# Prefix log-sum-exp over a sequence: all loads and stores issued by ScalarE instead of SyncE

## The chip, the cores and the metric

The kernel runs on one core of one Trainium2 chip. The metric is the device time of one execution in microseconds (us). The core has engines that each work through an instruction list of their own: TensorE (PE, with its weight loads as PEld), VectorE (DVE), ScalarE (ACT), GpSimd (POOL) and SyncE (SP). Transfers between the chip's memory (DRAM) and the buffers on the core are issued by an engine and carried out by 16 DMA engines. All numbers come from the times of whole executions and from one execution taken by the hardware profiler.

## The reference

For an input `x` of shape 4 x 4096 x 4128 (batch, sequence, features; float32), the output at each place is the logarithm of the sum of the exponentials of all inputs up to that place in the sequence:

```python
out[:, 0, :] = x[:, 0, :]
for t in range(1, S):
    mx = np.maximum(out[:, t - 1, :], x[:, t, :])
    out[:, t, :] = mx + np.log(np.exp(out[:, t - 1, :] - mx) + np.exp(x[:, t, :] - mx))
```

Input and output are 270.5 MB each.

## The kernel before

The kernel takes Exp of the input, makes a running sum over the sequence, and takes Ln of it. If a running sum leaves the safe range, a flag sends it to a slow general version (`_general`), which the profiled execution does not enter.

**Steps.** The sequence of each batch is cut into steps of `P * r` = 128 x 3 or 128 x 2 rows: each of the 128 partitions holds `r` consecutive rows of 4128 features. There are 45 steps, numbered 0 to 44 here (`n = 45`); 38 have three rows (6192 KB in and as much out) and seven have two (4128 KB): steps 0, 16, 27, 37, 39, 43 and 44. There are four buffers (`SLOTS = 4`); step t works in place in buffer t mod 4, so load t must wait until store t - 4 has landed.

**Chunks.** Each step is worked in three chunks of 1376 columns, 0 to 2. For a chunk, ScalarE takes Exp of all rows (`exp`, line 126); VectorE adds the rows of a partition (`sums`, lines 154 and 164); TensorE multiplies by a triangular matrix of ones, which gives each partition the sum over all partitions before it (`head`, line 172); VectorE adds that to the rows (`add`, lines 182, 188 and 197), and ScalarE takes Ln (`log`, lines 203, 207 and 208). What the steps before have summed up enters through the last partition, and for chunk 2 by `fold` (line 144).

**Order.** The order on each engine is written out by hand, under a manual schedule: `lists` holds one list of operations each for the moves, ScalarE (`act`), VectorE (`vec`) and TensorE (`pe`). `turns` says how many Exp of step t + 1 stand ahead of each Ln of step t. In most steps the ScalarE order is Ln chunk 0, two Exp of the next step, Ln chunk 1, the third Exp, Ln chunk 2. For step 40 all three Exp of step 41 stand ahead of the third Ln; after it come Ln of step 41 chunk 0, Exp of step 42 chunks 0 and 1, and so on.

**Moves.** The list `moves` (lines 228 to 237) is SyncE's: loads 0 to 3, store 0, store 1, load 4, store 2, load 5, and so on, store t followed by load t + 3; behind store 40 stand two loads, 43 and 44. A load is one transfer, except that loads 1, 2 and 3 (`BY_ROW`) are three each, one per row (line 107). This makes 96 transfers. The loop from line 345 to the end of the schedule emits the lists; `needs` says what an operation depends on, and `seen` which of its dependences an earlier wait has already covered. ScalarE's function tables are loaded at the start (line 37).

Of the kernel before, what the change touches and what calls it, by code (L numbers as in the profile page):

```python
# [13 lines left out]
MM = 512  # L14
NC = 3
SLOTS = 4
BY_ROW = (1, 2, 3)
PASSED = NC - 1
SMALL = 2.0 ** -63
LARGE = 2.0 ** 62  # L20
# [4 lines left out]
def kernel(  # L25
# [5 lines left out]
    nc = tc.nc  # L31
# [2 lines left out]
    CH = D // NC  # L34
    cuts = [(s, min(s + MM, CH)) for s in range(0, CH, MM)]

    nc.scalar.preload_act_table_set("natural_log_exp_and_others")
    consts = ctx.enter_context(tc.tile_pool(name="consts", bufs=1))
    zpool = ctx.enter_context(tc.tile_pool(name="zpool", bufs=1))
    xpool = ctx.enter_context(tc.tile_pool(name="xpool", bufs=1))  # L40
# [7 lines left out]
        out=below, in_=below, pattern=[[1, P]], compare_op=ALU.is_ge,  # L48
# [5 lines left out]
        out=carried, in_=below, pattern=[[0, P]], compare_op=ALU.not_equal,  # L54
# [4 lines left out]
        out=summed, in_=below, pattern=[[1, P]], compare_op=ALU.not_equal,  # L59
# [27 lines left out]
    made = {}  # L87

    def follows(inst, *ops):
        for op in ops:  # L90
            for other in made.get(op, ()):
                tc.declare_no_dep(inst.ins, other.ins, reason="a wait in between has seen it")

    class Step:
# [7 lines left out]

        def load(self):
            if self.n not in BY_ROW:
                return [nc.sync.dma_start(out=self.xt, in_=self.dram(x))]
            return [
                nc.sync.dma_start(out=self.xt[:, j, :], in_=self.dram(x)[:, j, :])
                for j in range(self.r)
            ]

        def store(self):
            return [nc.sync.dma_start(out=self.dram(out), in_=self.xt)]  # L112

    class Chunk:
        def __init__(self, step, c):
# [35 lines left out]
        def sums(self):  # L151
            r, e, got = self.t.r, self.row, []
            if r == 3:
                got.append(nc.vector.tensor_tensor(out=e[1], in0=e[0], in1=e[1], op=ALU.add))  # L154
                for free in () if self.passed else made.get(("log", self.t.n - 1, self.c), ()):
                    tc.add_manual_dep(
                        got[0].ins, free.ins.name,
                        mybir.DependencyInfo(
                            mybir.DependencyClass.Sync, mybir.DependencyReason.DATA,
                        ),  # L160
                        reason="the next sum writes what this Ln reads",
                    )
            n = P if self.passed else P - 1
            got.append(nc.vector.tensor_tensor(  # L164
                out=self.z[0:n], in0=e[r - 2][0:n], in1=e[r - 1][0:n], op=ALU.add,
            ))
            return got
# [46 lines left out]
    steps = []  # L214
# [10 lines left out]
        s.chunks = [Chunk(s, c) for c in range(NC)]  # L225
    n = len(steps)

    moves = [("load", t) for t in range(SLOTS)]
    ahead = SLOTS
    for t in range(n):  # L230
        moves.append(("store", t))
        if t and ahead < n:
            moves.append(("load", ahead))
            ahead += 1
            if ahead == n - 1:
                moves.append(("load", ahead))
                ahead += 1

    lists = {"move": moves, "act": [], "vec": [], "pe": []}
    act, vec, pe = lists["act"], lists["vec"], lists["pe"]  # L240
    usual_turn = (0, 2, 3, 3), (0, 0, 1, 1)
    alone = (0, 0, 0, 0)
# [15 lines left out]
    }  # L258
    given = {"exp": [0] * n, "sums": [0] * n}

    def exps(t, k):
        while t < n and given["exp"][t] < k:
            act.append(("exp", t, given["exp"][t]))
            given["exp"][t] += 1

    def passing(t):
        if t and steps[t - 1].last:
            vec.append(("total", t - 1, PASSED))
        if t < n:
            vec.append(("least" if steps[t].first else "fold", t, PASSED))  # L270

    def sums(t, k):
        while t < n and given["sums"][t] < k:
# [3 lines left out]
            if c == PASSED - 1 and t:  # L277
                passing(t)

    exps(0, 2)  # L280
    for t in range(n):
        ahead_exps, ahead_sums = turns.get(t, usual_turn)
        exps(t, NC)
        sums(t, 2)
        for c in range(NC):
            exps(t + 1, ahead_exps[c])
            act.append(("log", t, c))
            sums(t + 1, ahead_sums[c])
            vec.append(("add", t, c))
            if c == 0:  # L290
                sums(t, NC)
            pe.append(("head", t, c))
        exps(t + 1, ahead_exps[NC])
        sums(t + 1, ahead_sums[NC])
    passing(n)

    def needs(what, t, c=None):
        if what == "load":
            return [("store", t - SLOTS)]
        if what == "store":  # L300
            return [("log", t, c) for c in range(NC)]
        if what == "head":
            u, d = divmod(t * NC + c - 2, NC)
            need = [("sums", t, c), ("add", u, d)]
            if d == PASSED and u >= 0:
                need.append(("total", u, d) if steps[u].last else ("fold", u + 1, d))
            return need if c == PASSED else need + [("add", t - 1, c)]
        if what == "sums":
            need = [("exp", t, c)]
            if c != PASSED:  # L310
                return need + [("log", t - 1, c)]
            return need if steps[t].first else need + [("fold", t, c)]
        if what == "add":
            need = [("head", t, c)]
            return need + ([("least", t, PASSED)] if steps[t].first and t else [])
        return {
            "exp": [("load", t)],
            "fold": [("exp", t, c), ("head", t - 1, c)],
            "total": [("head", t, c)],
            "least": [("exp", t, c)],  # L320
            "log": [("add", t, c)],
        }[what]

    def seen(what, t, c=None):
        gone = [
            (op, u, d) for u in range(t % SLOTS, t, SLOTS) for d in range(NC)
            for op in ("exp", "least", "fold", "sums", "head", "add", "log")
        ]
        gone += [("load", u) for u in range(t % SLOTS, t, SLOTS)]
        gone += [("store", u) for u in range(t % SLOTS, t - SLOTS, SLOTS)]  # L330
        if what == "load":
            return gone
        gone.append(("store", t - SLOTS))
        if what == "exp":
            return gone
        gone.append(("load", t))
        if what == "store":
            gone += [(op, t, d) for d in range(NC) for op in ("exp", "least", "fold", "sums", "head", "add")]
        if what in ("head", "add", "log"):
            gone.append(("exp", t, c))  # L340
        if what in ("add", "log"):
            gone.append(("sums", t, c))
        return gone

    done, at = set(), {e: 0 for e in lists}
    while any(at[e] < len(l) for e, l in lists.items()):
        before = len(done), sum(at.values())
        for e, l in lists.items():
            while at[e] < len(l):
                op = l[at[e]]  # L350
                if op[1] < n:
                    if any(0 <= d[1] and d not in done for d in needs(*op)):
                        break
                    done.add(op)
                    of = steps[op[1]]
                    made[op] = getattr(of if len(op) == 2 else of.chunks[op[2]], op[0])()
                    for inst in made[op]:
                        follows(inst, *seen(*op))
                    if op[0] == "sums" and op[2] != PASSED:
                        for inst in made[op]:  # L360
                            follows(inst, *((o, op[1] - 1, op[2]) for o in ("sums", "head", "add")))
                        for inst in made[op][1:]:
                            follows(inst, ("exp", *op[1:]), ("log", op[1] - 1, op[2]))
                at[e] += 1
        assert before != (len(done), sum(at.values()))
# [3 lines left out]
        out=fits[:, :counts], in0=probe, scalar1=LARGE, scalar2=None, op0=ALU.is_le,  # L369
    )  # L370
    nc.vector.tensor_scalar(
        out=fits[0:1, counts:], in0=short, scalar1=SMALL, scalar2=None, op0=ALU.is_ge,
# [7 lines left out]
        out=flag, in0=good, scalar1=float(P), scalar2=None, op0=ALU.is_lt,  # L380
# [62 lines left out]
```

## Time and profile before

| what | value |
|---|---|
| time, median of 3 runs (lowest to highest) | 1260.25 us (1260.09 to 1260.42) |
| time of the profiled execution | 1259.65 us |
| its span, first to last instruction | 1257.9 us |
| DMA, mean over the span | 430 GB/s, 541.24 MB |
| busy DVE / ACT / PE | 1048.3 / 930.1 / 585.0 us |
| ACT waits for DVE `z`, line 207 | 168.1 us, 48 times |
| ACT waits for loads, line 126 | 124.1 us, 31 times, longest 11.0 |
| load of three rows, issue to landing, median | 40.1 us |
| store of three rows, issue to landing, median | 26.0 us |

The page has a line for each DMA queue (packets, MB, share of the 16 engines), and a map in which each digit is the busy share of one fortieth of the span in tenths. The chain of waits goes back from the last instruction, at each step to what released it. A row of the waits has the engine, its line, what it waited for, the total in us, the number of times and the longest. A row of the order of time has start and duration in us, engine, line, operation, output and input, the count of merged instructions, and in brackets the idle time before it and what ended that. A merged row's duration runs from the start of the first to the end of the last, with what lies between. "SPq" is SyncE's queue of transfers: the duration is that of the issue, not of the transfer.

### The profile page before, as it was taken

Reading aid. Unit: us, or ns where it says so; the run is one execution under the profiler, and the core shown is the slowest. Engines: PE = TensorE matmul, PEld = TensorE weight load, DVE = VectorE, ACT = ScalarE, POOL = GpSimd, SP = SyncE. Lnnn points to the kernel's source line nnn. Section 1 sums busy time; section 2 is a strip of 40 time slices with the busy share of each in tenths; the row PEclk is TensorE's granted clock in tenths of the full one; section 3 lists DMA queues with packets and bytes.
Section 4 is the critical chain, followed back from the end, with each engine's and each line's share of the span. In section 5 each row is a group of like instructions: output and inputs, shape, how many; then the busy total and the mean of one; then the engine's idle time right before and its main releaser. Section 6 shows DMA issues by size and latency. Waiting matters only on the chain.

```text
span 1257.9 us, 2769 instructions
## 1 busy us (share of the span) xinstructions
PE 585.0 (47%) x812; PEld 226.3 (18%) x812; DVE 1048.3 (83%) x534; ACT 930.1 (74%) x367; POOL 3.8 (0%) x16
## 2 busy tenths in 40 slices
PE   3465544445544463345444545345444545444452
PEld 1121211111111121112111112111111112111121
DVE  3998977888988797788898879778889879788894
ACT  6986777777777776777777767687777767687792
POOL 1000000000000000000000000000000000000000
PEclk9756776666666667666666667665666667567686
DMA  9999999999999999999999999999999999999998
GB/s 399 424 435 435 432 428 427 435 438 433 432 430 437 429 441 426 439 432 432 432 438 433 432 428 436 431 436 433 436 434 433 430 433 431 432 441 431 429 440 357
DMA packets 13838, 541.24 MB, mean 430 GB/s; under 512 B 1536, under 2 KB 1536, under 8 KB 1536
## 3 DMA queue, kind: packets, MB, share of 16 engines
q1 hardware_dynamic: 13824, 541.07, 99.7%
q8 instruction: 6, 0.10, 0.0%
q14 instruction: 8, 0.07, 0.0%
HBM read 270.53 MB, written 270.53 MB: 430 GB/s over the span
## 4 chain that ended last, share of the span: by engine, by line
DMA 62%; ACT 26%; DVE 9%; PE 1%; issue 0%; SPq 0%; ACTq 0%
DMA x<-in_x_dram 52%; ACT x L126 15%; DMA out_dram<-x 10%; ACT x L203 5%; ACT x L207 4%; DVE x L188 2%; ACT x L208 2%; DVE x L182 2%; DVE z L164 1%; DVE z L197 1%; DVE x L154 1%; DVE x L144 1%; PE p L172 1%; DVE x L164 0%; SPq L112 0%
## 5 line engine op out<-in xcount | busy, mean ns | idle before, releaser
L172 PE MATMUL p<-z,carried 128*128 128x512 f32 (+1 forms) x492 | 357.5, 890 | 452.2 <-DVE z L164 301.8
L126 ACT ACTIVATE x<-x 128x4128 f32<-128x4128 f32 (+1 forms) x135 | 461.5, 3452 | 124.2 <-DMA x<-in_x_dram 124.1
L207 ACT ACTIVATE x<-x 128x2752 f32<-128x2752 f32 (+1 forms) x90 | 208.1, 2312 | 181.1 <-DVE z L197 168.1
L154 DVE TENSOR_TENSOR x<-x 128x1376 f32<-128x1376 f32 x114 | 180.9, 1587 | 153.8 <-ACT x L126 153.8
L172 PE MATMUL p<-x,summed 128*128 128x512 f32 (+1 forms) x270 | 193.4, 879 | 142.9 <-DVE x L164 142.9
L172 PEld LDWEIGHTS p<-z,carried 128*128 128x128 f32 x492 | 138.7, 301 | 672.3 <-DVE z L164 337.4
L188 DVE TENSOR_TENSOR x<-p,x 128x2752 f32<-128x2752 f32 (+1 forms) x90 | 250.9, 2788 | 2.4 <-PE p L172 2.0
L182 DVE SCALAR_TENSOR_TENSOR x<-p,inner,x 128x4128 f32<-128x4128 f32 (+1 forms) x45 | 193.0, 4288 | 2.3 <-PE p L172 2.3
L164 DVE TENSOR_TENSOR z<-x 127x1376 f32<-127x1376 f32 x90 | 143.2, 1591 | 20.7 <-ACT x L126 18.1
L203 ACT ACTIVATE x<-x 128x4128 f32<-128x4128 f32 (+1 forms) x45 | 155.3, 3450 | 4.0 <-DVE x L182 4.0
L197 DVE TENSOR_TENSOR z<-x 128x1376 f32<-128x1376 f32 x82 | 130.6, 1592 | 2.8
L172 PEld LDWEIGHTS p<-x,summed 128*128 128x128 f32 x270 | 73.8, 291 | 259.9 <-DVE x L164 171.8
L208 ACT ACTIVATE x<-z 128x1376 f32<-128x1376 f32 x90 | 120.0, 1333 | 0.0
L164 DVE TENSOR_TENSOR x<-x 128x1376 f32<-128x1376 f32 x45 | 71.6, 1591 | 1.3
L144 DVE TENSOR_TENSOR x<-p,x 1x1376 f32<-1x1376 f32 x41 | 64.7, 1577 | 7.9 <-ACT x L126 7.9
L172 PE MATMUL p<-z,below 128*128 128x512 f32 (+1 forms) x48 | 34.8, 892 | 54.4 <-DVE z L164 41.9
L172 PEld LDWEIGHTS p<-z,below 128*128 128x128 f32 x48 | 13.7, 304 | 75.4 <-issue 32.6
L136 DVE TENSOR_REDUCE short<-x 1x1 f32<-1x4128 f32 x3 | 13.3, 4429 | 0.0
L191 DVE CUSTOM_DVE_ANT_0 z<-x 128x1376 f32<-128x1376 f32 x8 | 12.7, 1592 | 0.3
L147 DVE TENSOR_REDUCE probe<-p 1x1 f32<-1x1376 f32 x4 | 6.3, 1571 | 0.0
L129 ACT ACTIVATE x<-x,twice 1x1376 f32<-1x1376 f32 x3 | 4.3, 1442 | 0.2
L377 PE MATMUL good<-ones,low 128*1 128x1 f32 x2 | 0.2, 164 | 5.5 <-DVE low L375 5.5
(23 smaller groups left out, 7.9 us busy)
## 6 DMA issues: line engine op xcount, KB each, us to landing
out_dram<-x SPq DMA_DIRECT2D x38, 6192.0 KB, 26.0
x<-in_x_dram SPq DMA_DIRECT2D x35, 6192.0 KB, 40.1
x<-in_x_dram SPq DMA_DIRECT2D x7, 4128.0 KB, 35.2
out_dram<-x SPq DMA_DIRECT2D x7, 4128.0 KB, 25.9
x<-in_x_dram SPq DMA_DIRECT2D x9, 2064.0 KB, 34.4
```

What stands on the lines that cost most here:

```text
L126: got = [nc.scalar.activation(self.e, self.e, ACT.Exp)]
L136: return [nc.vector.tensor_reduce(out=short[:, self.t.b - 1:self.t.b], in_=self.t.xt[0:1, 0, :], op=ALU.min, axis=AX.X,)]
L144: return [nc.vector.tensor_tensor(out=to, in0=pt[0:1], in1=to, op=ALU.add)]
L154: got.append(nc.vector.tensor_tensor(out=e[1], in0=e[0], in1=e[1], op=ALU.add))
L164: got.append(nc.vector.tensor_tensor(out=self.z[0:n], in0=e[r - 2][0:n], in1=e[r - 1][0:n], op=ALU.add,))
L172: nc.tensor.matmul(self.pt[:, a:b], lhsT=w, rhs=self.z[:, a:b], start=True, stop=True,)
L182: return [nc.vector.scalar_tensor_tensor(out=self.e, in0=base, scalar=inner[:, 0:1], in1=self.e, op0=ALU.mult, op1=ALU.add,)]
L188: got = [nc.vector.tensor_tensor(out=e, in0=base, in1=e, op=ALU.add)]
L197: nc.vector.tensor_tensor(out=self.z, in0=ends[0], in1=ends[1], op=ALU.add)
L203: return [nc.scalar.activation(self.e, self.e, ACT.Ln)]
L207: nc.scalar.activation(e, e, ACT.Ln),
L208: nc.scalar.activation(self.row[r - 1], self.z, ACT.Ln),
```

## The change

Every load and store is issued by ScalarE. Loads 0 to 3 are emitted ahead of the loop over the lists, and the load of ScalarE's tables comes behind them. The list of moves is gone; the stores and loads stand in ScalarE's list: store t behind the third Ln of step t, and load t + 3 right behind store t, from t = 2 on; load 4 stands behind the second Exp of step 3; load 44 stands behind load 43, both behind store 40. What each operation depends on is not changed. Load 3 becomes one transfer, so that the run has 94.

```diff
-BY_ROW = (1, 2, 3)
+BY_ROW = (1, 2)
...
-    nc.scalar.preload_act_table_set("natural_log_exp_and_others")
...
         def load(self):
             if self.n not in BY_ROW:
-                return [nc.sync.dma_start(out=self.xt, in_=self.dram(x))]
+                return [nc.scalar.dma_start(out=self.xt, in_=self.dram(x))]
             return [
-                nc.sync.dma_start(out=self.xt[:, j, :], in_=self.dram(x)[:, j, :])
+                nc.scalar.dma_start(out=self.xt[:, j, :], in_=self.dram(x)[:, j, :])
                 for j in range(self.r)
             ]
 
         def store(self):
-            return [nc.sync.dma_start(out=self.dram(out), in_=self.xt)]
+            return [nc.scalar.dma_start(out=self.dram(out), in_=self.xt)]
...
-    moves = [("load", t) for t in range(SLOTS)]
-    ahead = SLOTS
-    for t in range(n):
-        moves.append(("store", t))
-        if t and ahead < n:
-            moves.append(("load", ahead))
-            ahead += 1
-            if ahead == n - 1:
-                moves.append(("load", ahead))
-                ahead += 1
-
-    lists = {"move": moves, "act": [], "vec": [], "pe": []}
+    lists = {"act": [], "vec": [], "pe": []}
...
+    due = []
+
     def exps(t, k):
         while t < n and given["exp"][t] < k:
             act.append(("exp", t, given["exp"][t]))
             given["exp"][t] += 1
+            if due and given["exp"][t] == due[0][1]:
+                act.append(("load", due.pop(0)[0]))
...
             pe.append(("head", t, c))
+        act.append(("store", t))
+        if t == 1:
+            due.append((SLOTS, 2))
+        elif t and t + SLOTS - 1 < n - 1:
+            act.append(("load", t + SLOTS - 1))
+            if t + SLOTS == n - 1:
+                act.append(("load", n - 1))
         exps(t + 1, ahead_exps[NC])
...
     done, at = set(), {e: 0 for e in lists}
+    for t in range(SLOTS):
+        made["load", t] = steps[t].load()
+        done.add(("load", t))
+    nc.scalar.preload_act_table_set("natural_log_exp_and_others")
```

## The prediction

> **What bounds the kernel now.** First the page: the share of the DMA queue and the map of slices.
>
> ```profile
> span 1257.9 us, 2769 instructions
> DMA  9999999999999999999999999999999999999998
> q1 hardware_dynamic: 13824, 541.07, 99.7%
> DMA 62%; ACT 26%; DVE 9%; PE 1%; issue 0%; SPq 0%; ACTq 0%
> ```
>
> The 16 DMA engines work through all 40 slices: the kernel is a stream of 541.07 MB, and only what makes a hole in that stream, or lengthens its two ends, can cost time. The chain of waits (last line) agrees: 62% in transfers. Then I looked at what SyncE's queue waits for, and at its issues in order of time.
>
> ```profile
> SPq L112 <- ACT x L203: 1116.9, 45, 32.2
> SPq L105 <- DMA out_dram<-x: 65.6, 11, 23.9
> 381.35 0.33 SPq L112 DMA_DIRECT2D out_dram<-x  x1
> 381.78 0.38 SPq L105 DMA_DIRECT2D x<-in_x_dram  x1
> 410.60 0.33 SPq L112 DMA_DIRECT2D out_dram<-x  x1
> ...
> 1086.24 0.34 SPq L105 DMA_DIRECT2D x<-in_x_dram  x1
> ...
> 1163.86 0.33 SPq L112 DMA_DIRECT2D out_dram<-x  x1
> 1164.29 24.64 SPq L105 DMA_DIRECT2D x<-in_x_dram  x2
> 1191.83 0.34 SPq L112 DMA_DIRECT2D out_dram<-x  x1
> ```
>
> A step issues one store and one load every 29.25 us (410.60 - 381.35); that is 12.68 MB, or 433.5 GB/s. SyncE waits 1117 us for the last Ln of a step, and eleven times, 65.6 us in all, for an old store to land before it may overwrite its buffer. The longest of these, 23.9 us, is the second of the two loads from 1164.29: load 44, issued at 1188.6, which wants the buffer of store 40, itself issued only at 1163.86. SyncE can afford it, since nothing stands behind it until store 41 at 1191.83. Last I read ScalarE around that moment and VectorE where it takes over.
>
> ```profile
> 413.25 2.50 ACT L207 ACTIVATE x<-x 128x2752 f32<-128x2752 f32 x1 [2.67 <-DVE z L197]
> 1160.19 3.64 ACT L203 ACTIVATE x<-x 128x4128 f32<-128x4128 f32 x1
> 1166.49 2.50 ACT L207 ACTIVATE x<-x 128x2752 f32<-128x2752 f32 x1 [2.66 <-DVE z L197]
> 1168.89 1.33 ACT L208 ACTIVATE x<-z 128x1376 f32<-128x1376 f32 x1
> 1173.94 7.18 ACT L126 ACTIVATE x<-x 128x4128 f32<-128x4128 f32 x2 [3.71 <-DMA x<-in_x_dram]
> 1177.61 1.59 DVE L154 TENSOR_TENSOR x<-x 128x1376 f32<-128x1376 f32 x1 [3.47 <-ACT x L126]
> 1237.81 2.50 ACT L203 ACTIVATE x<-x 128x2752 f32<-128x2752 f32 x1 [0.41 <-DVE x L182]
> ```
>
> While SyncE waits from 1164.7 to 1188.6, ScalarE does the Ln of step 41 and the Exp of step 42, and from 1177.61 VectorE runs with hardly a gap to 1237.8; then the last Ln, the last store (issued 1240.33) and its landing.
>
> **The change, part by part.** *Loads 0 to 3 on ScalarE, ahead of the table load.* Eight transfers instead of ten (1 + 3 + 3 + 1). The by-row issues on SyncE took 0.33 to 0.51 us, the first 0.39. No row shows an issue on ScalarE; bounded by nothing (if it costs ScalarE no time) and the 1.28 us of the table load, I take SyncE's 0.33 to 0.45, the same kind of instruction. 8 x 0.45 = 3.6 us from 0.80, then the table load of 1.28: ready at about 5.7. The first Exp waits for load 0 until 13.09, so this is hidden; without that cover it would cost 4.9. The first issue stays at 0.80.
>
> *Load 3 whole.* In the trace its second and third rows were issued at 13.09 and 17.98, when the first and the second transfer landed: eight were in flight. Now there are eight in all and no such wait. The bytes are the same and the stream is full, so what it can give is a better rate: the second slice ran 424 GB/s against 433.5, or 31.4 x 9.5 / 433.5 = 0.7 us. Bounds 0 and -0.7; I take 0.
>
> *Load 4* moves from behind store 1 to behind the second Exp of step 3. It was issued at 67.74, when store 0 landed; the Exp run from 62.97 puts it at 62.97 + 0.5 + 3 x 3.55, about 74. Store 1, issued at 63.1, needs 14.6 us of stream after store 0 (landed 67.7), so the stream lasts to about 81 and load 4 still joins it in time: 0. If store 1 were not there, 6 us.
>
> *45 stores and 41 later loads on ScalarE.* Each pair takes 0.33 + 0.38 and 0.1 between them (381.35 to 382.16), and ScalarE must first let its Ln end, 0.1: 0.9 us, right behind the last Ln of a step. The next ScalarE instruction, the first Ln of the next step, waits 2.67 us for VectorE there (413.25), so 0.9 is covered; uncovered, it would be 45 x 0.9 = 40 us of ScalarE, still inside the stream's 29.25 us a step, of which ScalarE works some 21 (930.1 / 45). SyncE's queue has nothing left, POOL's is not touched. Sum 0, save one place in the tail: store 42 comes ahead of an unbroken ScalarE run, which feeds VectorE within 0.1 us at 1224.9: +0.45.
>
> *The waits that move along.* That is the price. A load that waits for its buffer now holds up ScalarE's own list: Exp and Ln stand behind it, VectorE's sums behind these, then the next store. Of 65.6 us, 4.2 was load 4's. Nine waits sum to 65.6 - 4.2 - 23.9 = 37.5 us, up to 8.2 us (load 40). What covers them is the transfers outstanding: a load lands a median 40.1 us after issue, and the next store is issued 28.8 us after it, so 11.3 us remain, less about 2.5 between data and landing (load 0: 12.3 us for 4.23 MB, which is 9.75 us of stream): 8.8 us. The three worst delays are each a wait plus the 0.9 of the issues: 5.9 + 0.9 = 6.8 us before store 18, 5.5 + 0.9 = 6.4 before store 29, and 8.2 + 0.9 less an old wait of 1.35 for load 39, 7.7, before store 38, where load 40, awaited at 1120.3 and so 9.9 after that store, leaves a cover of 9.9 - 2.5 = 7.4. Between them ScalarE gains its waits on loads back, some 4.9 us a step. So 0 at the first two, 0 to +1.5 at the third: I take +0.7. If the cover were gone, all 37.5 us would be paid.
>
> *Load 44* has no such cover. ScalarE stands from 1164 (or, 6 us late, 1170) until store 40 lands at 1188.5, a time set by the stream and not by ScalarE. Then: issue, 1189.0; Ln of step 41, 3.64; the Exp of step 42 starts at 1192.7 where it was 1173.94: **18.7 us late**. VectorE, which followed that Exp from 1177.61 without slack, is late by the same, and so is every later store; store 44 goes out at 1240.33 + 18.7 + 0.45 = 1259.5. In the trace the stream was full to about 1253 and store 44, behind other stores, landed 16.5 us after its issue; now the last four stores find holes (21.1 MB, 48.8 us of stream, would have started at about 1205; store 41 comes at 1210.5), and store 44 finds the queue nearly empty: 12.3 us, the row of load 0, of the same size. It lands at 1271.8, and with the 1.1 us that now follow the landing the span is 1272.9, or +15.0. Bounds: 9.75 us of pure stream for the landing gives +12.4, the 16.5 us row +19.2.
>
> Sum against the profiled execution, 1259.65 (span 1257.9 and 1.75 around it): 1259.65 + 15.0 + 0.7 = 1275.4. It ran 0.6 under the median of the runs, 1260.25; carried to the median: **1276.0**.
>
> **Rivals.** *The short waits drain the stream too*: the cover is nearer 5 us than 8.8, as a sum at the mean rate suggests (at 433.5 GB/s the bytes issued before 410.60 end 4.6 us after it). Then the three places lose 1.8 + 1.4 + 2.7, in all 6 instead of 0.7: 1276.0 + 5.3, about 1282. Against it: loads land 40.1 us after issue and not the 35.7 of that sum, so some of the 16 engines run behind the mean, and these set the landing.
>
> *The waiting load does not hold ScalarE*, a waiting transfer being passed by Exp and Ln. Then the stream has no hole, the issues are hidden, and the time is 1260.25 less at most 0.7: 1260, not slower. It decides once load 44's wait holds ScalarE for less than about 10 us: of the 24.7 from 1164.3 to 1189.0, all but 15.0 is taken up by the old waits of 2.66 and 3.71 and the faster landing of store 44. For it: no row shows ScalarE behind its own issue. Against it: on SyncE, store 0 and rows 2 and 3 of load 3 went strictly one behind the other's wait. The Trainium skill ("DMA: Bandwidth & Descriptors", section "Issuing engines are not separate DMA queues") says that transfers end on the same 16 engines whoever issues them, and that the issuer changes only the sequencer's issue time. By that rule alone the sum would also be 0 and the time 1260; the trace agrees with it as far as one queue at 99.7% goes, but the rule does not count what is queued behind the waits.
>
> *A better rate*: the stream runs at 436 instead of 433.5 GB/s, with the tail as forecast: 541.07 MB in 1241.0 instead of 1248.1 us, 7 us less, about 1269. For it: slices of 435 to 441; against it: before has one queue and the same pieces too.
>
> *The edit doesn't do what it says*, the waits being met elsewhere: 1260.
>
> **Numbers.** Forecast 0.73, with its own range 1270 to 1281; drained stream 0.13; not held 0.08; better rate 0.04; no effect 0.02. The measurement tells 0.2%, 2.5 us, from no change. Slower: forecast, drained stream and better rate, 0.90. Of the 0.10 for not held and no effect, 0.08 is same and 0.02 faster, in case the better rate joins them (1260 - 7). The range takes in the drained stream, the far end of the landing row, and VectorE's two waits for TensorE in the tail (4.65 and 4.97 us for six matmuls that took 2.58 at 93.25, so up to 4.5 less if the rest leaves it a better clock): 1267 to 1286.
>
> **What would show it.** ScalarE idle for 18 to 25 us in one piece near 1165 to 1189, ended by store 40's landing, with load 44's issue at its end; DMA share falling below 0.9 in two or three places after 1205; eight or nine shorter stops of ScalarE of 1 to 8 us; loads of the usual steps still landing near 40 us. I am wrong if Ln of step 41 runs during load 44's wait, if ScalarE issues take well over 0.5 us, or if the mean rate before 1160 departs from 433.

## The result and the profile after

The changed kernel takes 1280.92 us (median of 6 runs, 1278.78 to 1281.91) against 1260.17 for the kernel before on the same chips: a ratio of 1.0163, with a 95% interval of 1.0150 to 1.0177, or **20.7 us slower**. The profiled execution took 1278.78 us, the lowest of the six, with a span of 1277.0.

The page of the changed kernel first: the map of the DMA engines, the GB/s by slices, the queue.

```profile
span 1277.0 us, 2720 instructions
DMA  9999999999999999999999999999999999999968
GB/s 398 429 432 432 430 434 434 430 433 434 433 431 432 435 435 431 434 430 422 430 439 430 435 431 436 432 432 427 419 424 444 424 437 434 440 390 424 395 298 364
q10 hardware_dynamic: 13536, 541.07, 98.6%
```

The same bytes go over one queue, now ScalarE's. The stream runs at its old rate where nothing stops it. It has shallow dips near slices 19 and 29 (422 and 419 GB/s; the kernel before has no slice under 424 between its first and its last), deeper ones from slice 36 on, and a real hole in slice 39, at 298 GB/s. ScalarE's waits (what it waited for, total, times, longest) say what is new:

```profile
ACT x L125 <- DMA x<-in_x_dram: 89.3, 21, 8.5
ACT x L125 <- DMA out_dram<-x: 33.7, 6, 6.9
ACT x L206 <- DMA out_dram<-x: 23.0, 1, 23.0
```

ScalarE never waited for a store before. Now its Exp and Ln do, seven times, 56.7 us in all, because a load listed ahead of them waits for its buffer; its waits for loads shrink from 124.1 to 89.3 us in part payment. Around the longest, ScalarE in order of time, and then VectorE in the same place:

```profile
1168.15 3.63 ACT L202 ACTIVATE x<-x 128x4128 f32<-128x4128 f32 x1
1171.81 0.34 ACTq L111 DMA_DIRECT2D out_dram<-x  x1
1172.19 22.57 ACTq L104 DMA_DIRECT2D x<-in_x_dram  x2
1194.80 2.50 ACT L206 ACTIVATE x<-x 128x2752 f32<-128x2752 f32 x1 [23.02 <-DMA out_dram<-x]
...
1216.33 0.35 ACTq L111 DMA_DIRECT2D out_dram<-x  x1
...
1264.61 0.34 ACTq L111 DMA_DIRECT2D out_dram<-x  x1
```

```profile
1180.51 1.59 DVE L196 TENSOR_TENSOR z<-x 128x1376 f32<-128x1376 f32 x1
1202.10 1.59 DVE L153 TENSOR_TENSOR x<-x 128x1376 f32<-128x1376 f32 x1 [20.00 <-ACT x L125]
```

Store 40 goes out at 1171.81, load 43 right behind it, load 44 only when store 40 has landed; until then ScalarE does nothing, and VectorE, short of the Exp of step 42, stands 20 us. Store 41, 28 us behind store 40 in the kernel before, now follows after 44.5. Two stretches of that time show the price, first in the changed kernel and then in the kernel before (start:end, length, then busy time and instructions of PE, PEld, DVE, ACT and POOL, granted clock, DMA share, GB/s):

```profile
1210.00:1215.00 5.00, 0.90 (x2) 0.50 (x2) 4.97 (x4) 5.00 (x2) 0.00 (x0) 0.50 0.15 66
...
1230.00:1235.00 5.00, 2.45 (x5) 0.80 (x3) 5.00 (x3) 5.00 (x3) 0.00 (x0) 0.81 0.37 159
```

```profile
1210.00:1215.00 5.00, 3.90 (x5) 1.83 (x6) 4.96 (x4) 5.00 (x2) 0.00 (x0) 0.50 0.94 406
...
1230.00:1235.00 5.00, 4.33 (x9) 1.67 (x7) 4.55 (x5) 2.45 (x3) 0.00 (x0) 0.76 0.93 400
```

The DMA engines, 0.94 and 0.93 busy in the kernel before, are nearly empty ahead of store 41 (0.15) and slack again ahead of store 42 (0.37).

The six shorter stops work in the same way. Here load 20 waits for store 16, and the store that comes after the stop goes out late. ScalarE in the changed kernel first, then SyncE in the kernel before; the store is store 18 in both:

```profile
514.78 10.71 ACT L125 ACTIVATE x<-x 128x4128 f32<-128x4128 f32 x3 [4.79 <-DMA out_dram<-x]
...
553.22 0.34 ACTq L111 DMA_DIRECT2D out_dram<-x  x1
```

```profile
547.07 0.33 SPq L112 DMA_DIRECT2D out_dram<-x  x1
```

### The profile page after: what moved, and what is told of

Same layout as the page of the kernel before. It is cut to its first block, busy times and chain, and to the rows that moved or that the text cites. A ratio compares the mean times of both kernels' runs of the same rounds, so it can differ in the third digit from the quotient of the medians.

```text
span 1277.0 us, 2720 instructions
## 1 busy us (share of the span) xinstructions
PE 579.5 (45%) x812; PEld 225.4 (18%) x812; DVE 1047.4 (82%) x534; ACT 929.8 (73%) x367; POOL 3.8 (0%) x16
## 4 chain that ended last, share of the span: by engine, by line
DMA 49%; ACT 34%; DVE 15%; ACTq 1%; issue 0%
DMA x<-in_x_dram 36%; ACT x L125 21%; DMA out_dram<-x 13%; ACT x L202 5%; ACT x L206 5%; DVE x L187 5%; DVE z L196 3%; ACT x L207 3%; DVE x L181 2%; DVE x L143 2%; DVE x L163 1%; DVE z L163 1%; DVE x L153 1%; ACTq L111 0%; DVE z L190 0%
## 5 line engine op out<-in xcount | busy, mean ns | idle before, releaser
L125 ACT ACTIVATE x<-x 128x4128 f32<-128x4128 f32 (+1 forms) x135 | 461.5, 3452 | 125.3 <-DMA x<-in_x_dram 89.3
L171 PE MATMUL p<-x,summed 128*128 128x512 f32 (+1 forms) x270 | 189.8, 865 | 151.2 <-DVE x L163 151.2
L171 PE MATMUL p<-z,below 128*128 128x512 f32 (+1 forms) x48 | 33.7, 864 | 55.2 <-DVE z L163 42.1
```

The costliest lines, as they stand in the source:

```text
L125: got = [nc.scalar.activation(self.e, self.e, ACT.Exp)]
L171: nc.tensor.matmul(self.pt[:, a:b], lhsT=w, rhs=self.z[:, a:b], start=True, stop=True,)
```

## The experiments

Theory H: the loss is what stands behind waiting loads in ScalarE's list. Rivals: I, the issues themselves cost ScalarE time on the path; Q, its queue is slower. The kernel before was run beside each group of runs, and ratios are against it.

**Load 44 back on SyncE.**

```diff
-                return [nc.scalar.dma_start(out=self.xt, in_=self.dram(x))]
+                by = nc.sync if self.n == n - 1 else nc.scalar
+                return [by.dma_start(out=self.xt, in_=self.dram(x))]
```

> The changed kernel with load 44 alone back on SyncE. Theory H (waits held in ScalarE's list are the whole loss, load 44's about 15 us of the 20.7, the short waits the rest): 1281 - 15 = 1266, between 1263 and 1269; ScalarE's 23 us stop near 1172 is gone, the shorter stops before loads 17, 20, 28, 31, 38 and 40 stay. Rival I (each of the 88 issues on ScalarE costs about 0.2 us of the path): 1280. Rival Q (ScalarE's queue moves the bytes more slowly): 1280.

Measured: 1266.96 us, ratio 1.0055 (1.0040 to 1.0070). ScalarE's longest wait for a store is 6.9 us in its profile. So load 44's place was worth 1280.92 - 1266.96 = 14.0 us, and 6.8 us remain, which the prediction had put at 0.7. I and Q are out for the larger part.

**Loads 43 and 44 alone on ScalarE**, all else as before.

```diff
-                return [nc.sync.dma_start(out=self.xt, in_=self.dram(x))]
+                by = nc.scalar if self.n >= n - 2 else nc.sync
+                return [by.dma_start(out=self.xt, in_=self.dram(x))]
...
+        if t + SLOTS == n - 1:
+            act.append(("load", n - 2))
+            act.append(("load", n - 1))
```

> The kernel before with loads 43 and 44 alone issued by ScalarE, at the place that they have in the changed kernel, all else on SyncE. H: ScalarE stands some 24 us from about 1164 until store 40 lands, and the time is 1260 + 15 = 1275, between 1272 and 1279. I: two issues cost under 1 us, 1261. Q: two of 96 transfers on the other queue, 1261.

Measured: 1283.24 us, ratio 1.0182 (1.0166 to 1.0198): the sign that H gives, but 8 us more. The rows of this kernel, ScalarE's and then SyncE's:

```profile
1161.02 0.38 ACTq L106 DMA_DIRECT2D x<-in_x_dram  x1
1161.82 3.63 ACT L204 ACTIVATE x<-x 128x4128 f32<-128x4128 f32 x1
1199.97 0.33 ACTq L106 DMA_DIRECT2D x<-in_x_dram  x1
```

```profile
1165.47 105.83 SPq L113 DMA_DIRECT2D out_dram<-x  x5
```

ScalarE issued load 43 at 1161.02, ahead of the last Ln of step 40, so it was in flight before store 40 (1165.47), which then took 34.5 us to land instead of 24.7. The 9.8 us between them are what load 43's 4.23 MB take at 433.5 GB/s (9.75). ScalarE stood 34.9 us. The expectation had overlooked that SyncE's store and ScalarE's load no longer keep their order.

**Two tiny transfers a step on ScalarE**, the kernel before else.

```diff
...
+        def tiny(self):
+            return [
+                nc.scalar.dma_start(
+                    out=told[0:16, 16 * k:16 * k + 16], in_=self.xt[0:16, self.r - 1, D - 16:D],
+                )
+                for k in range(2)
+            ]
...
+        act.append(("tiny", t))
...
```

> The kernel before with two transfers of 1 KB each (16 partitions x 64 bytes, inside the core) added to ScalarE's list behind the last Ln of every step: ScalarE issues 90 transfers, and none of them waits for an old transfer to land. H: 1260, within 2 us, the issues hidden in ScalarE's idle time. I: a good part of the 20 us, 1268 or more. Q says nothing here.

Measured: 1261.65 us, ratio 1.0013 (1.0004 to 1.0022): 1.5 us (0.5 to 2.8) for 90 issues and the 2880 packets that they add. Not all of it need be ScalarE's: in this kernel SyncE's stores waited five times, 29.0 us in all, for a tiny transfer to land, which the expectation had not foreseen. A step of that kernel shows where they go: right behind the last Ln, ahead of a Ln that waits for VectorE as it did before.

```profile
377.31 3.63 ACT L212 ACTIVATE x<-x 128x4128 f32<-128x4128 f32 x1
380.97 1.16 ACTq L117 DMA_DIRECT2D told<-x  x2
383.61 2.50 ACT L216 ACTIVATE x<-x 128x2752 f32<-128x2752 f32 x1 [2.67 <-DVE z L206]
```

The idle time before the Ln of line 216 is 2.67 us, to the digit what it was without them.

**Everything on ScalarE, seven loads further down its list.** Load 4 keeps its place.

```diff
+    later = {4: (3, 2), 17: (15, 3), 20: (18, 2), 28: (26, 3), 31: (29, 2), 38: (36, 3), 40: (38, 3), n - 1: (n - 3, 3)}
+
+    def load(t):
+        if t in later:
+            due.append((t, *later[t]))
+        else:
+            act.append(("load", t))
...
-            if due and given["exp"][t] == due[0][1]:
+            if due and (t, given["exp"][t]) == due[0][1:]:
                 act.append(("load", due.pop(0)[0]))
...
         if t == 1:
-            due.append((SLOTS, 2))
+            load(SLOTS)
         elif t and t + SLOTS - 1 < n - 1:
-            act.append(("load", t + SLOTS - 1))
+            load(t + SLOTS - 1)
             if t + SLOTS == n - 1:
-                act.append(("load", n - 1))
+                load(n - 1)
```

> The changed kernel, everything issued by ScalarE, but loads 17, 20, 28, 31, 38, 40 and 44 stand further down its list, behind one to three Exp, about where their store has landed (load 44 behind the third Exp of step 42). H: no stop of ScalarE for a landing longer than 2 us or so and 1260 to 1263. I: 1279 to 1281, as the number of issues is the same. Q: 1279 to 1281 too.

Measured: 1260.04 us against 1260.13, ratio 0.9999 (0.9990 to 1.0008). The whole loss is gone with all 94 transfers on ScalarE, so neither their number nor the queue costs more than about 1 us, the upper end of that interval. Its queue line and ScalarE's only wait for a store:

```profile
q10 hardware_dynamic: 13536, 541.07, 99.6%
ACT x L202 <- DMA out_dram<-x: 0.7, 1, 0.7
```

**The same, with load 44 behind load 43 again** (its entry in `later` taken out).

> The changed kernel with loads 17, 20, 28, 31, 38 and 40 further down ScalarE's list, as in the run before, but load 44 right behind load 43, as in the change. If the two parts add up (load 44 14.0, as its move to SyncE gave, and the short waits 6.8): 1260 + 14 = 1274, between 1272 and 1276, with one stop of ScalarE of about 23 to 25 us. If they feed each other: 1270 or less, or 1278 or more.

Measured: 1273.47 us, ratio 1.0107 (1.0092 to 1.0123): 13.5 us for load 44 alone, so the parts add up, 13.5 + 6.8 = 20.3 of 20.7. Its rows are those that the prediction worked out without the short waits:

```profile
1163.77 24.68 ACTq L104 DMA_DIRECT2D x<-in_x_dram  x2
1188.51 2.50 ACT L206 ACTIVATE x<-x 128x2752 f32<-128x2752 f32 x1 [25.14 <-DMA out_dram<-x]
```

Store 44 landed 11.1 us after its issue, where the prediction had taken 12.3: most of the 1.5 us by which its 15.0 was too high. Beside the run of loads 43 and 44 on ScalarE: a stop of 25.1 us cost 13.5, one of 34.9 cost 23.1; 9.8 us more of stop, 9.6 us more of time.

**Load 3 whole, the kernel before else** (`BY_ROW = (1, 2)`).

> The kernel before with load 3 as one transfer, nothing else. The prediction's term: 0, bounds 0 to -0.7, so 1259.4 to 1260.2. Rival: the whole load holds back the two before it or store 0, +1 or more.

Measured: 1259.91 us against 1259.92, ratio 1.0000 (0.9991 to 1.0009). Load 3 is out of the matter, to within about 1.1 us.

**How much a store may be late.** To the version with the later loads, a hold of ScalarE ahead of the third Ln of steps 5, 8, 11, 20 and 31; `TIMES` is 8 or 20.

```diff
...
+        def hold(self):
+            return [nc.scalar.activation(spare, spare, ACT.Relu) for k in range(TIMES)]
...
+            if c == PASSED and t in HELD:
+                act.append(("hold", t, c))
             act.append(("log", t, c))
...
```

> The version with the later loads, with ScalarE held at five quiet places (steps 5, 8, 11, 20 and 31) ahead of the third Ln by eight small Relu over a spare tile (128 x 400), some 3.4 to 4.2 us each, so that five stores go out that much late. With a cover of 5 us, as with one of 8.8: 1260, within 1.5 us. With no cover: 1260 + 17 or more.

> The same with twenty Relu, 8.6 to 10.4 us at each of the five places. Cover of 8.8 us, as the prediction took it: 1260 to 1268. Cover of 5: the stream loses 3.6 to 5.4 at each place, 18 to 27 in all, so 1278 to 1287.

Measured: 1263.89 us (ratio 1.0026, 1.0016 to 1.0037; eight runs from 1261.71 to 1265.88) and 1286.57 us (1.0213, 1.0197 to 1.0229). ScalarE's rows at step 5, of the first and of the second kernel, give the holds:

```profile
171.34 4.50 ACT L139 ACTIVATE spare<-spare 128x400 f32<-128x400 f32 x8
175.75 3.63 ACT L209 ACTIVATE x<-x 128x4128 f32<-128x4128 f32 x1
```

```profile
170.80 11.32 ACT L139 ACTIVATE spare<-spare 128x400 f32<-128x400 f32 x20
182.02 3.63 ACT L209 ACTIVATE x<-x 128x4128 f32<-128x4128 f32 x1
```

A store 4.4 us late (175.75 - 171.34) costs (1263.89 - 1260.04) / 5 = 0.8 us; one 11.2 us late costs (1286.57 - 1260.04) / 5 = 5.3. The interval of the first run makes its 0.8 us 0.4 to 0.9. The first expectation missed: the small hold was not free. The second run lies in the range given for a cover of 5 us and far above that for 8.8; but its holds were longer than expected, and at 11.2 us a sharp cover of 5 would have cost 6.2 a place, one of 8.8 only 2.4, against the 5.3 measured. So the cover is near 5 to 6 us and wears out by degrees. On the line between the two points, 6.8 us of delay cost 0.8 + (6.8 - 4.4) x 4.5 / 6.8 = 2.4; that the loss is a line between them is an assumption.

## Why the prediction was right, and which term was too small

It forecast 1276.0, slower, in a range of 1267 to 1286; measured were 1280.92. The mechanism was the one named, and one term of the sum was mis-sized.

- **Load 44: right.** The term was +15.0; moving that load alone measured 14.0 and 13.5, so it was 1.0 to 1.5 too high and hid that much of the next term's miss. Without the short waits ahead of it, ScalarE went on at 1188.5 (worked out: 1189.0, after the issue) and store 44 went out at 1259.61 (worked out: 1259.5).
- **The short waits: too small, and the source of the miss.** The prediction put +0.7; measured were 6.8. Of the nine waits that it counted (37.5 us) six were left as stops, 33.7 us. The delays that it priced were right in sum: 6.8, 6.4 and 7.7 us had been worked out for stores 18, 29 and 38, and the trace has 6.4, 7.4 and 6.7, each against the drift of the quiet stores ahead of it (store 18 at 553.22 against 547.07, with store 14 already 0.3 ahead; store 29 at 867.66 against 859.38, with store 22 0.9 behind; store 38 at 1120.56 against 1110.43, with store 34 3.4 behind). That drift grows from -0.3 to 0.9 over the first of these places and to 3.4 over the second.
- **The step that failed: the cover.** The prediction let a store be some 8.8 us late at no cost, a figure taken from median landings less 2.5. The holds show a loss from 4.4 us on and about 2.4 at 6.8, three times which is 7.2. The first rival had this: a cover near 5 us, from the mean rate, 5.9 us in all and 1282. (The prediction gave the third place 1.4 us less cover than the others, 7.4 against 8.8; carried into the rival, that makes 4.1 there instead of 2.7, and 7.3 in all.)
- **What may lie behind it.** The trace records the landing of a transfer in 16 parts. In the kernel before they come 3.6 us apart (median, first to last). The load issued at 381.78 shows the 11.3 us of the prediction (421.93 - 410.60); its last part landed at 421.93, its first at 418.28. So a part of the stream has up to 3.6 us less in hand than the last part tells, 8.8 - 3.6 = 5.2. This fits a loss that begins near 4.4 us and grows by degrees; no run varied it.
- **Lateness alone does not set the price.** Stores 15, 26 and 36, each behind another of the six stops, were 5.4, 6.6 and 5.4 us late by the same count, about as late as store 18. The prediction did not price them, and no loss shows behind them: the next store landed no later, against the kernel before, than the store ahead of the late one (within 0.1 us). Behind stores 18, 29 and 38 the next store landed 1.0, 1.5 and 2.8 us later. What differs is the load in flight: when stores 15, 26 and 36 went out it had some 7.0 us left to its landing, at stores 18 and 29 5.0, at store 38 2.2. So the stream began to lose with between 5 and 7 us left to a landing, where the prediction allowed 2.5.
- **No cost of issue: right.** Where ScalarE waited for nothing else, ahead of the Exp at 116.94, store and load took 0.91 us out of its time, as worked out; at a usual step they lie inside a wait for VectorE of 2.67. The version with the later loads bounds the sum at about 1 us.
- **Load 3, the table load, load 4: right at 0.** The table load ran at 4.83, long before the first Exp at 13.00. Load 4 went out at 67.91, not at 74 as worked out (below).
- **The rivals.** "Does not hold ScalarE" is out: ScalarE stood 23.0 us. The rule of the Trainium skill that stood beside it ("DMA: Bandwidth & Descriptors", section "Issuing engines are not separate DMA queues"), that the issuer changes only the issue time, holds for this kernel where no long wait stands in the list (1260.04 with everything on ScalarE and one wait of 0.7 us for a store) and not for the list as the change wrote it. "A better rate" is out: 430 GB/s without stops, as before.
- **The clock: nothing to gain.** The range allowed up to 4.5 us less, from "VectorE's two waits for TensorE in the tail". That reading was wrong: 4.65 and 4.97 us are the lengths of two groups of six matmuls in the chain, during which VectorE worked; it waited for TensorE once there, 0.4 us. The granted clock was 0.50 from 1210 to 1215, after ScalarE's stop, and from the first Exp of step 42 to the last store the tail took 66.2 us, against 66.4 in the kernel before.

## What to carry to other kernels

A transfer that waits for a buffer holds up whatever stands behind it on its issuer: nothing on an engine that does only transfers, the whole chain on one that computes. Before moving transfers to a computing engine, list their waits one by one, by length and by what stands behind; of a wait that is long against the work outstanding in the DMA queue, all but a fixed part is paid (here all but 11.6 and 11.8 us of stops of 25.1 and 34.9), and the load is best moved down the list to where the transfer it waits for has landed. Take the outstanding work from bytes at the mean rate, not from the landing time of single transfers: the shorter figure (4.6 us against 8.8) was the nearer one here.

## What had not been expected of the hardware

ScalarE's issue of a transfer is not held until the activations ahead of it have run. Load 4 stands behind the second Exp of step 3, but in the changed kernel it went out before that Exp began:

```profile
63.37 7.18 ACT L125 ACTIVATE x<-x 128x4128 f32<-128x4128 f32 x2 [0.43 <-ACT x L202]
67.91 0.35 ACTq L104 DMA_DIRECT2D x<-in_x_dram  x1
70.45 3.63 ACT L125 ACTIVATE x<-x 128x4128 f32<-128x4128 f32 x1
```

The two merged Exp end at 70.55 and the Exp that the load stands behind starts at 70.45, 2.5 us after the load's issue. So the issue runs ahead of work already listed, as load 43 did in the experiment above; only work listed behind a waiting transfer is held. The other surprise is what the order of two queues does. In the run of loads 43 and 44 on ScalarE, store 40, issued 4.5 us after a 4.23 MB load on the other queue, took 9.8 us longer to land; that is the whole of the load's 9.75 us, so the price was that of being behind it, and not of a second queue. In the run with load 44 alone on SyncE a later transfer held up an earlier one: load 43, on ScalarE's queue from 1172.27, landed 15.8 us after store 40, where it had been 9.75 in the kernel before, with load 44 issued on the other queue at 1195.10; ScalarE's Exp of step 43 waited 6.2 us for it.
